# Encoder trunk on one core: other PSUM banks for one projection, another order of SBUF pools, another tail, and the inverse ahead of the stacks

## The chip, the cores and the metric

The kernel runs on one core of a Trainium2 chip. Its engines work side by side, each through its own list of instructions in order: TensorE (PE; the loading of its weights is shown apart as PEld), VectorE (DVE), ScalarE (ACT), GpSimd (POOL) and SyncE (SP), which only issues transfers. ACT and POOL issue transfers too. The metric is the time of one execution on the device in microseconds (us); lower is better.

## What is computed

A trunk of two layers over 1024 frames of width 1024, in float32. Layer 0 mixes by a recurrence (RWKV-7, 8 heads of 64) and by chunked band attention (8 heads of 64); layer 1 is a Conformer convolution module. Each layer ends with an MLP of squared ReLU, and the whole with an RMSNorm.

```python
for layer in range(DEPTH):
    h = rmsnorm(x, mix_norms[layer])
    if layer % 2 == 0:
        x = x + rwkv_attention_mixer(h, *mix_params[layer])
    else:
        x = x + conformer_conv(h, *mix_params[layer])
    g_ffn, up, down = ffn_params[layer]
    x = x + sq_relu_mlp(rmsnorm(x, g_ffn), up, down)
return rmsnorm(x, final_norm)
```

The mixer projects once for both groups; the recurrence holds a 64 x 64 state for each head, and the attention has a window of its own chunk and the eight before it:

```python
def step(S, inp):
    r_t, w_t, k_t, v_t, kk_t, a_t = inp
    sa = jnp.einsum('bhij,bhj->bhi', S, -kk_t)
    S = (S * w_t[:, :, None, :]
         + sa[..., None] * (kk_t * a_t)[:, :, None, :]
         + v_t[..., None] * k_t[:, :, None, :])
    y = jnp.einsum('bhij,bhj->bhi', S, r_t)
    return S, y
```

## The kernel before

**Layout.** Activations lie transposed, channels on the 128 partitions and frames along the row. The frames are worked in two halves of T = 512 (half 0 and half 1), each as 8 tiles of 128 x 512. Every large product is done in three steps for one: both operands are split into a rounded part and a rest (`xh` and `xl`, `wh` and `wl`), and `xh*wh`, `xl*wh` and `xh*wl` are summed in PSUM. All these steps go through `dense` (L141, matmul at L144). Weights come from memory as `wr` (L250, four buffers), ACT rounds them to `wh` (L258) and DVE takes the difference `wl` (L259); `wh` and `wl` have the four buffers of pool `wp1` in the narrow part of the kernel and the eight of `wp2` in the wide part.

**Who sets the order.** A planner (the tile framework) lays out each engine's list when the kernel is built. It takes instructions that are ready by its own estimate of time, the one with the lowest priority number first. `At(name)` sets the class: "support" before "mixer" (the recurrence), "mixer" before "attn", "attn" before "dense". Dense steps thus fill what the others leave; they come in runs (`run_of`; 6 in the projections, 12 in the narrow MLP) whose later steps follow their head at once. A tile of a pool can be written when the planner has seen the release of the buffer's last user, and memory of a closed pool is reused by the pools opened after it, tile by tile.

**PSUM.** The narrow part has eight banks by name: d 2, w 2, v 1, c 1, a 2 (L1095). "d" is for the dense products, "w" for the preparation of the recurrence, "v" for its stacks and inverse, "c" for its chain, "a" for attention. The wide part has d 5, w 1, o 2 (L1161).

**Order of stages.** Input projection of half 0 (`w_in_gemm(0)`); then recurrence and attention of half 0 beside the input projection of half 1 (`w_in_gemm(1)`); then recurrence and attention of half 1 beside output projection and MLP of layer 0 for half 0. From L1159 on the kernel is wide: `glu(0)`, the convolution of half 0, `mixer_out(1)` and the MLP of half 1, and so on through layer 1; the last call is `ffn(xb, ...)` with the writer `Out(1, xb, up, True)`.

**Value projection.** The end of `w_in_gemm` (L421 to L437) makes the attention's values with frames on the partitions: four banks at once, one for each 128 frames, over eight steps of weights. The banks are those of `SPARE` (L266): d, d, a, a. In both halves; with half 0 "a" is free, with half 1 attention(0) uses "a" too.

**Recurrence.** A unit is a pair of heads in a block of 256 frames, eight units to a half. `prep` makes its operands, among them `bk` (keys and the like) and `vp` (values); in half 1 (`nbuf` = 2) there is one buffer of each, and also of `bkt` and `vs`. `stacks` (L698) turns `bk` on PE through bank "v" and copies it to `bkt` (L705, L706), then centres the values, also through "v", into `vs` (L710, L715). `invert` (L631) inverts four triangular 64 x 64 blocks: on DVE (L638 to L653), with two writes to and eight reads from DRAM on SP's queue (L660, L667), then by 16 and three times 16 small matmuls through bank "v" (L676, L688) into `xt`. `stage2` does the stacks, then the inverse, then `late`. `chain` (L725) walks through four chunks: it needs `xt`, `bkt` and `vs`. The loop of `rwkv` (L454 to L467) traces stage 3 of one unit, stage 2 of the next and stage 1 of the one after in turns.

**Wide pools.** L1161 opens, one above the other, `wp2` (split weights, 32 KB a partition), `mp2` (MLP's middle, 40 KB), `sx` (16 KB) and `up` (convolution: `dwt`, `halo`, `u`, `cv` and others, some 43 KB). Below them lay, from the bottom, `lop` and `wp1` (26 KB), `mp` (32 KB), and the pools of the recurrence and the attention of half 1.

**Tail.** `Out.add` runs behind each 128-channel tile of the last down product: ACT scales a copy (L1053), PE turns it back (L1059), ACT and DVE copy it to the output rows `u` (L1065, L1067). `Stat.add` squares each tile on ACT (L220) and adds it on DVE (L221). With the last tile, which is done in two halves of 256 frames, `write` (L1075) sums the squares over the partitions on PE (L1079), takes root and reciprocal (L1082, L1083), scales the output rows (L1089 on ACT, L1091 on DVE) and stores them from SP's queue (L1092).

## Time and profile before

| | us |
|---|---|
| median of 3 runs (lowest, highest) | 2415.16 (2414.27, 2418.61) |
| the profiled execution, its own time | 2409.59 |
| its span, first to last instruction | 2407.5 |
| PE busy in it | 2374.8 |
| DVE, ACT, POOL busy | 1706.2, 1198.9, 117.1 |
| mean granted TensorE clock | 0.998 |

A row of a table by line has: line, engine, operation, names out<-in, shapes, count, then busy us, mean ns of one, idle us of the engine just before, and what ended that idle time. A row in order of time has: start, length, engine, line and names, in brackets the idle time before. Rows of waits have: who waited, for whom, us in total, times, longest. A matmul's length is longer than its share of PE's time, since the next one starts before it ends; starts are what counts.

### The profile page before, as it was taken

The numbers are of one execution on the slowest core, as the hardware profiler recorded it, in microseconds if no ns is written. First come the engines' busy times: TensorE is split into PE (matmuls) and PEld (weight loads), VectorE is DVE, ScalarE is ACT, GpSimd is POOL, SyncE is SP. The second block draws the span as 40 slices with busy tenths as digits, with TensorE's granted clock in tenths as the row PEclk, the third lists the DMA queues.
The fourth block names the chain that finished last, engine by engine and source line by source line (L and its number), as shares of the span: only waits on it lengthen the run. The fifth ranks groups of instructions, "written<-read, shape, count | busy, mean of one in ns | idle before, by whom it ended". The sixth has DMA issues, their size and how long they took to land.

```text
span 2407.5 us, 37122 instructions
## 1 busy us (share of the span) xinstructions
PE 2374.8 (99%) x12804; PEld 1956.4 (81%) x12804; DVE 1706.2 (71%) x3575; ACT 1198.9 (50%) x2323; POOL 117.1 (5%) x243
## 2 busy tenths in 40 slices
PE   9999999899999999999999999999999999999998
PEld 7777777788888888888888888888888888888887
DVE  6787776587777764579999746799997465434434
ACT  6567666677676753434433335334333365423324
POOL 1120111100000000011000000000000000000000
PEclk9999999999999999999999999999999999999999
DMA  8574445633343323453333334433333334333332
GB/s 260 163 217 139 120 121 171 188 102 115 93 120 110 90 74 90 145 166 92 101 97 97 97 97 135 123 94 97 96 98 99 95 112 140 97 97 97 97 98 67
DMA packets 476042, 283.34 MB, mean 118 GB/s; under 512 B 44512, under 2 KB 453216, under 8 KB 475856
## 3 DMA queue, kind: packets, MB, share of 16 engines
q1 hardware_dynamic: 464976, 249.46, 35.7%
q0 software_dynamic: 9488, 30.28, 3.6%
q8 instruction: 101, 1.65, 0.3%
q10 hardware_dynamic: 1392, 1.24, 0.2%
q14 instruction: 85, 0.70, 0.1%
HBM read 247.31 MB, written 36.72 MB: 118 GB/s over the span
## 4 chain that ended last, share of the span: by engine, by line
PE 88%; DVE 4%; DMA 3%; ACT 3%; issue 1%; SPq 1%; ACTq 0%; DVEq 0%
PE d L144 77%; DMA pt<-pd 1%; PE a L160 1%; PE v L688 1%; PE a L883 1%; DVE wl L259 1%; PE a L144 1%; ACT wh L258 1%; PE a L861 1%; PE a L863 1%; PE c L746 1%; PE c L740 0%; DVE pr L650 0%; PE c L736 0%; PE v L676 0%
## 5 line engine op out<-in xcount | busy, mean ns | idle before, releaser
L258 ACT CAST wh<-wr 128x512 fp32r<-128x512 f32 x744 | 460.1, 620 | 922.9 <-PE d L144 839.0
L144 PE MATMUL d<-xh,wh 128*128 128x512 f32 x1872 | 745.6, 398 | 0.3 <-DVE t L408 0.2
L144 PE MATMUL d<-xh,wl 128*128 128x512 f32 x1872 | 730.7, 391 | 0.9 <-DVE wl L259 0.9
L144 PE MATMUL d<-xl,wh 128*128 128x512 f32 x1872 | 730.2, 390 | 0.0
L259 DVE TENSOR_TENSOR wl<-wr,wh 128x512 fp32r<-128x512 f32 x744 | 503.4, 687 | 197.5 <-ACT wh L258 142.2
L144 PEld LDWEIGHTS d<-xh,wl 128*128 128x128 f32 x1872 | 351.7, 188 | 76.4 <-DVE wl L259 1.3
L144 PEld LDWEIGHTS d<-xh,wh 128*128 128x128 f32 x1872 | 352.2, 188 | 70.0 <-issue 1.2
L144 PEld LDWEIGHTS d<-xl,wh 128*128 128x128 f32 x1872 | 352.3, 188 | 67.7 <-issue 0.5
L144 PE MATMUL d<-mh,wh 128*128 128x512 f32 (+1 forms) x1040 | 405.8, 390 | 0.0
L144 PE MATMUL d<-mh,wl 128*128 128x512 f32 (+1 forms) x1040 | 401.8, 386 | 0.0
L144 PE MATMUL d<-ml,wh 128*128 128x512 f32 (+1 forms) x1040 | 401.6, 386 | 0.0
L1014 DVE SCALAR_TENSOR_TENSOR cv<-u,dwt,cv 128x512 f32<-128x512 f32 x480 | 332.7, 749 | 0.7
L144 PEld LDWEIGHTS d<-mh,wl 128*128 128x128 f32 x1040 | 195.4, 188 | 40.0
L144 PEld LDWEIGHTS d<-ml,wh 128*128 128x128 f32 x1040 | 195.6, 188 | 37.6
L144 PEld LDWEIGHTS d<-mh,wh 128*128 128x128 f32 x1040 | 195.5, 188 | 37.7
L913 DVE TENSOR_TENSOR x<-d,x 128x512 f32<-128x512 f32 (+1 forms) x146 | 97.8, 681 | 152.1 <-PE d L144 151.6
L955 DVE SCALAR_TENSOR_TENSOR t<-d,rstd 128x512 f32<-128x512 f32 x128 | 86.6, 688 | 114.6 <-PE d L144 111.9
L961 DVE TENSOR_TENSOR ml<-t,mh 128x512 fp32r<-128x512 f32 x128 | 87.9, 689 | 12.6 <-ACT mh L959 9.5
L957 ACT ACTIVATE t<-t 128x512 f32<-128x512 f32 x128 | 80.0, 625 | 12.2 <-DVE t L955 11.2
L959 ACT ACTIVATE mh<-t 128x512 fp32r<-128x512 f32 x128 | 78.9, 616 | 0.0
L745 ACT ACTIVATE sd<-vs,dc 64x64 f32<-64x64 f32 x128 | 44.1, 345 | 40.7 <-DVE vs L749 29.6
L221 DVE TENSOR_TENSOR acc<-acc,t 128x512 f32<-128x512 f32 (+1 forms) x86 | 58.0, 675 | 8.4 <-ACT t L220 8.3
(271 smaller groups left out, 2335.0 us busy)
## 6 DMA issues: line engine op xcount, KB each, us to landing
wr<-in_up_dram SPq DMA_DIRECT2D x256, 256.0 KB
wr<-in_dn_dram SPq DMA_DIRECT2D x256, 256.0 KB
wr<-in_w_in_dram SPq DMA_DIRECT2D x103, 256.0 KB
wr<-in_pw_dram SPq DMA_DIRECT2D x96, 256.0 KB
wr<-in_w_out_dram SPq DMA_DIRECT2D x32, 256.0 KB
pd<-t POOLq DMA_DIRECT2D x28, 256.0 KB, 2.6
x<-xd SPq DMA_DIRECT2D x24, 256.0 KB
pt<-pd SPq DMA_DIRECT2D x42, 128.5 KB
```

The lines of the kernel that those rows point to most:

```text
L144: ins = nc.tensor.matmul(*a, **k)
L160: ins = issue(*a, **k)
L221: nc.vector.tensor_tensor(out=self.acc[:, cols], in0=self.acc[:, cols], in1=sq[:, cols], op=ALU.add)
L258: nc.scalar.copy(hi[:], raw[:])
L259: nc.vector.tensor_tensor(out=lo[:], in0=raw[:], in1=hi[:].bitcast(F32), op=ALU.subtract)
L745: nc.scalar.activation(sd[hs[hd], :], sv[hs[hd], hd, c, :], AF.Copy, scale=dc[hs[hd], c : c + 1])
L913: nc.vector.tensor_tensor(out=xs[m][:, cols], in0=q[:, cols], in1=xs[m][:, cols], op=ALU.add)
L955: nc.vector.scalar_tensor_tensor(out=t[:], in0=q[:], scalar=0.0, in1=rstd[:], op0=ALU.max, op1=ALU.mult)
L957: nc.scalar.activation(sq[:], t[:], AF.Square)
L959: nc.scalar.activation(hi[:], t[:], AF.Square)
L961: nc.vector.tensor_tensor(out=lo[:], in0=sq[:], in1=hi[:].bitcast(F32), op=ALU.subtract)
L1014: nc.vector.scalar_tensor_tensor(out=c[:], in0=u[:, tap : tap + T], scalar=dw(tap), in1=c[:], op0=ALU.mult, op1=ALU.add)
```

## The change

Four edits. (A) In half 1 the value projection takes the banks d, d, v, c. (B) With `nbuf` = 2, that is in half 1, `stage2` runs the inverse ahead of the stacks. (C) The wide part opens its pools as `up`, `mp2`, `sx`, `wp2`. (D) In the tail the sum of squares is moved out of `write` into `sums`, which can add several parts; with the last tile of the last writer the square is made on DVE, is not added to the accumulator but summed beside it on PE, and `sums` is traced ahead of the turning back. There three of the four rows of a half are scaled on DVE and one on ACT, and two of the four are stored from ACT's queue.

```diff
--- before.py
+++ after.py
@@ -419,7 +419,7 @@
         run_of(RUN[0])
         gemm(w_in, 0, IN_ORDER, rhs, evac, st, first, mark=h)
         run_of(RUN[2])
-        qs = [psum(tag) for tag in SPARE]
+        qs = [psum(tag) for tag in (SPARE if h == 0 else ("d", "d", "v", "c"))]
         for k in range(KT):
             with boost():
                 hi, lo = (a[:].rearrange("p a b -> p (a b)")
@@ -785,8 +785,12 @@
             nc.gpsimd.dma_start(yd[hp][:, t0 : t0 + RT], yc[:])
 
         def stage2(u):
-            yield from stacks(u)
-            yield from invert(u)
+            if nbuf > 2:
+                yield from stacks(u)
+                yield from invert(u)
+            else:
+                yield from invert(u)
+                yield from stacks(u)
             late(u)
 
         def stage3(u):
@@ -919,14 +923,19 @@
 
         gemm(w, row0, range(KT), rhs, evac, taper=taper, after=after, halves=halves)
 
-    def norm_collect(xs, gname):
+    def norm_collect(xs, gname, final=False):
         st = Stat()
         rhs = [None] * KT
 
         def last(m, cols):
             if gname is not None:
                 rhs[m] = split(xs[m][:], m, v(gname, m))
-            st.add(xs[m][:], cols)
+            if final and m == KT - 1:
+                sq = tmp("t2")
+                nc.vector.tensor_tensor(out=sq[:, cols], in0=xs[m][:, cols], in1=xs[m][:, cols], op=ALU.mult)
+                st.rest = sq
+            else:
+                st.add(xs[m][:], cols)
 
         return st, rhs, last
 
@@ -942,7 +951,7 @@
         return nrhs, st
 
     def ffn(xs, rhs, rst, up, dn, mp, nxt, out_to=None, late=None):
-        st, nrhs, last = norm_collect(xs, nxt)
+        st, nrhs, last = norm_collect(xs, nxt, out_to is not None and out_to.final)
         if out_to is not None:
             out_to.st = st
         groups = DFF // D
@@ -1051,9 +1060,11 @@
         def add(self, m, cols):
             n = tmp("t1")
             nc.scalar.activation(n[:, cols], self.xs[m][:, cols], AF.Copy, scale=v("gf", m))
-            q = psum("o")
             c2, j = divmod(m, 4)
             ts = range(cols.start // P, cols.stop // P)
+            if self.final and m == KT - 1:
+                self.sums([self.st.acc, self.st.rest], ts)
+            q = psum("o")
             for t in ts:
                 with At("dense"):
                     nc.tensor.transpose(q[:, t * P : (t + 1) * P], n[:, t * P : (t + 1) * P], ident)
@@ -1068,28 +1079,34 @@
             if self.final and m == KT - 1:
                 self.write(ts)
 
-        def finish(self):
-            with boost():
-                self.write(range(4))
-
-        def write(self, ts):
+        def sums(self, parts, ts):
             q = psum("o")
-            for t in ts:
+            pairs = [(part, t) for part in parts for t in ts]
+            for i, (part, t) in enumerate(pairs):
                 with At("dense"):
-                    nc.tensor.matmul(q[:, t : t + 1], self.st.acc[:, t * P : (t + 1) * P], ones[:, 0:1], start=True, stop=True)
+                    nc.tensor.matmul(q[:, t : t + 1], part[:, t * P : (t + 1) * P], ones[:, 0:1],
+                                     start=(i == 0), stop=(i == len(pairs) - 1))
             w = slice(ts[0], ts[-1] + 1)
             r = self.r
             nc.scalar.activation(r[:, w], q[:, w], AF.Sqrt, bias=kc[:, 0:1], scale=1.0 / D)
             nc.vector.reciprocal(out=r[:, w], in_=r[:, w])
-            for c2 in range(2):
-                for t in ts:
-                    rows = slice(self.h * T + t * P, self.h * T + (t + 1) * P)
-                    o = self.o[4 * c2 + t][:, 0:T]
-                    if t % 2:
-                        nc.scalar.activation(o, o, AF.Copy, scale=r[:, t : t + 1])
-                    else:
-                        nc.vector.tensor_scalar(o, o, r[:, t : t + 1], None, op0=ALU.mult)
-                    nc.sync.dma_start(out[rows, c2 * T : (c2 + 1) * T], o)
+
+        def finish(self):
+            with boost():
+                self.sums([self.st.acc], range(4))
+                self.write(range(4))
+
+        def write(self, ts):
+            r = self.r
+            for i, (c2, t) in enumerate((c2, t) for c2 in range(2) for t in ts):
+                rows = slice(self.h * T + t * P, self.h * T + (t + 1) * P)
+                o = self.o[4 * c2 + t][:, 0:T]
+                if i == 1 if self.final else t % 2:
+                    nc.scalar.activation(o, o, AF.Copy, scale=r[:, t : t + 1])
+                else:
+                    nc.vector.tensor_scalar(o, o, r[:, t : t + 1], None, op0=ALU.mult)
+                queue = nc.scalar if self.final and i in (1, 2) else nc.sync
+                queue.dma_start(out[rows, c2 * T : (c2 + 1) * T], o)
 
 
     with banks(d=2, w=2, v=1, c=1, a=2), tc.tile_pool(name="lop", bufs=1) as lop, tc.tile_pool(name="wp1", bufs=4) as wb[0]:
@@ -1158,7 +1175,7 @@
 
     wide[0] = True
     run_of(1)
-    with banks(d=5, w=1, o=2), tc.tile_pool(name="wp2", bufs=8, reuse_waits="tile") as wb[0], tc.tile_pool(name="mp2", bufs=10, reuse_waits="tile") as mp, tc.tile_pool(name="sx", bufs=4, reuse_waits="tile") as extra[0], tc.tile_pool(name="up", bufs=1, reuse_waits="tile") as up:
+    with banks(d=5, w=1, o=2), tc.tile_pool(name="up", bufs=1, reuse_waits="tile") as up, tc.tile_pool(name="mp2", bufs=10, reuse_waits="tile") as mp, tc.tile_pool(name="sx", bufs=4, reuse_waits="tile") as extra[0], tc.tile_pool(name="wp2", bufs=8, reuse_waits="tile") as wb[0]:
         dwt = up.tile([P, KT * TAPS], F32, tag="dwt", name="dwt")
         nc.scalar.dma_start(dwt[:], vecs[:, VOFF["dw"] : NVEC])
         halo = up.tile([P, KT, TAPS - 1], F32, tag="halo", name="halo")
```

## What was forecast before the run

> **What bounds the kernel now.** I read the page's busy times first, then the same by stretches, then the engines' order in time where a stretch shows idle TensorE, because an engine that is busy 99% of the span leaves only its idle time, and slow-clocked time, to win.
>
> ```profile
> span 2407.5 us, 37122 instructions
> PE 2374.8 (99%) x12804; PEld 1956.4 (81%) x12804; DVE 1706.2 (71%) x3575; ACT 1198.9 (50%) x2323; POOL 117.1 (5%) x243
> ```
>
> The table by stretches has start and end, length, busy time of PE, PEld, DVE, ACT and POOL with counts, the granted PE clock, DMA share and GB/s.
>
> ```profile
> 300.00:420.00 120.00, 117.41 (x910) 94.34 (x910) 85.46 (x288) 81.64 (x204) 17.16 (x39) 1.00 0.49 147
> 429.50:436.50 7.00, 6.48 (x31) 4.91 (x29) 2.31 (x5) 5.66 (x11) 1.08 (x2) 1.00 0.72 214
> 436.50:445.90 9.40, 5.31 (x41) 3.75 (x41) 2.12 (x9) 3.91 (x8) 0.54 (x1) 0.88 0.37 145
> 445.90:464.50 18.60, 17.88 (x76) 14.45 (x77) 12.53 (x25) 12.08 (x24) 3.18 (x12) 0.97 0.61 188
> 480.00:960.00 480.00, 476.51 (x3296) 393.05 (x3296) 341.52 (x978) 314.35 (x660) 18.04 (x52) 1.00 0.35 99
> 1028.50:2399.00 1370.50, 1370.45 (x6159) 1136.47 (x6157) 978.83 (x1566) 535.59 (x920) 26.08 (x24) 1.00 0.35 103
> ```
>
> From 1028.5 to 2399 us PE is idle for 0.05 us: 6159 matmuls in 1370.5 us, 0.2225 us each, and nothing but fewer matmuls could shorten that. In 480 to 960, where the recurrence and the attention of half 1 run with layer 0's MLP between them, only 3.5 us of 480 are idle. The hole is 436.5 to 445.9: 4.1 us of 9.4 are idle and the clock there is 0.88. So the change is worth what it does in three places: that hole, the seam to the wide part near 1027, and the tail after 2399.
>
> **Edit A, banks of the value projection in half 1.** In order of time (start, length, engine, line, in brackets the idle time before and what ended it):
>
> ```profile
> 436.55 0.88 PE L160 MATMUL a<-pT,vt 128*64 128x128 f32 x12 [0.57 <-ACT pT L884]
> 441.89 1.27 PE L883 MATMUL a<-cst,pt 128*128 128x128 f32 x8 [3.32 <-ACT pt L874]
> 443.88 1.97 PE L160 MATMUL a<-pT,vt 128*64 128x128 f32 x16 [0.73 <-ACT pT L884]
> 445.79 0.80 PE L144 MATMUL a<-wh,xh 128*128 128x512 f32 x1
> 446.38 0.63 PE L144 MATMUL a<-wh,xl 128*128 128x512 f32 x1
> 446.81 0.53 PE L144 MATMUL a<-wl,xh 128*128 128x512 f32 x1
> 447.17 0.39 PE L144 MATMUL a<-wh,xh 128*128 128x512 f32 x1
> ```
>
> PE waits three times for the last softmax of attention(0), and right behind it the value projection goes on in banks "a" (names in `a<-wh,xh`). It owns two "a" banks by its list and can't get them before attention(0) lets go; its two "d" banks had run ahead as far as the four buffers of split weights let them (24 of 48 steps before 436). In the changed list the other two banks are "v" and "c". Their users in half 0 are done earlier; the last reader of "c" there is the gate product (`e<-e,c`), and the first user of "v" in half 1 comes at 481.8.
>
> ```profile
> 427.78 0.42 DVE L784 TENSOR_TENSOR e<-e,c 128x256 f32<-128x256 f32 x1
> ...
> 481.80 0.55 PE L705 MATMUL v<-cst,bk 128*128 128x128 f32 x3
> ```
>
> So from 428.2 us all four banks are free, and 96 steps of 0.2225 us, 21.4 us of dense work that has the lowest priority, stand ready to fill the hole. Attention(0) itself ends no earlier: its steps are a chain through ACT and DVE.
>
> What goes: 0.57 + 3.32 + 0.73 = 4.62 us idle. And the clock: 0.12 x 9.4 + 0.03 x 18.6 = 1.7 us of lost clock in the two stretches. In rows: the 16 matmuls of 443.88 take 1.97 us where 12 took 0.88, so 16 should take 1.17: 0.8 lost; the three starts behind 445.79 are 0.59, 0.43 and 0.36 us apart instead of 0.2225: 0.7 lost. I take 1.5. Filling a hole is not perfect: with dense work at hand all the time, the stretch 300 to 420 still has 2.6 us of idle in 120, 0.022 per us, so 28 us (429.5 to 457.5) give 0.6 back. A = -(4.62 + 1.5) + 0.6 = **-5.5 us**; ends -6.1 and, if the planner places no step in the hole, 0.
>
> The Trainium skill ("TensorE: Matmul & The Clock Gate", Part 1: The HAM clock gate) says the array's clock falls to half after an idle window of about 3.4 us and returns after as long a busy one. The granted clock agrees here: the idle time was 3.32 us and 1.7 us of clock were lost behind it. Without that rule the sum would have the 4.62 us alone.
>
> What is late next: the projection ends near 464.5 - 6 = 458.5 instead of 464.5, and the output projection of half 0 must be ready to take over.
>
> ```profile
> 449.76 0.37 SPq L938 DMA_DIRECT2D mh<-yd  x1
> 465.92 0.69 DVE L189 TENSOR_TENSOR xl<-mh,xh 128x512 fp32r<-128x512 f32 x1 [0.38 <-ACT xh L188]
> ```
>
> ```profile
> pd<-t POOLq DMA_DIRECT2D x28, 256.0 KB, 2.6
> ```
>
> The last attention tile is reloaded at 449.8, and its split at 465.9 waits not for it but for the projection to free the eighth input buffer. With as long a way as the page gives for a 256 KB store, 2.6 us, it is there by 452.5, six us ahead of need. The casts and differences of the weights for the last four steps (4 x 1.3 us on ACT and DVE) now fall into the softmax and may put attention(0) back by 1 to 2 us; the 6 us cover that.
>
> **Edit B, the inverse ahead of the stacks in half 1.** No instruction is added or removed. The end of one unit's stacks (L710) and inverse (from L676), and then the next unit:
>
> ```profile
> 623.37 0.71 PE L710 MATMUL v<-cent,vp 128*128 128x128 f32 x4
> 628.88 0.68 PE L676 MATMUL v<-e,g 64*64 64x64 f32 x16
> 641.20 0.63 PE L705 MATMUL v<-cst,bk 128*128 128x128 f32 x4
> 666.32 0.44 DVE L670 STREAM_TRANSPOSE e<-xdt 128x256 f32<-128x256 f32 x1
> 676.77 0.38 PE L746 MATMUL c<-vs,bkt 128*128 128x128 f32 x2
> 677.38 0.59 ACT L706 COPY bkt<-v 128x512 f32<-128x512 f32 x1
> 685.34 0.68 PE L676 MATMUL v<-e,g 64*64 64x64 f32 x16
> ```
>
> The transposed keys sit in the only "v" bank from 641.2 to 678, because their copy needs the only buffer `bkt`, which the chain of the unit before reads until L746. The inverse has its input at 666.8 but starts on PE at 685.3. The inverse's ten DMAs (L660, L667) and its DVE part lie before 666 and wait for none of this, so SP's queue keeps its order; the stacks issue no DMA. What can move is 16 + 3 x 16 small matmuls, by up to 18.5 us, per unit. That shortens a latency of the recurrence, which is not what bounds the stretch: PE is full of dense matmuls there, and the recurrence ends 70 us before the dense work it hides behind (last stores of each):
>
> ```profile
> L785 POOL DMA_DIRECT2D yd<-e x16: 539/539/542, 164.7 to 957.3; - x16
> 1027.95 0.50 PE L144 MATMUL d<-xh,wl 128*128 128x512 f32 x1 [0.93 <-DVE wl L259]
> ```
>
> B = **0**; ends: -3.5 (all idle of 480 to 960 gone) and +3.5 (that idle doubled).
>
> **Edit C, order of the wide pools.** The second row above is the seam: the first split weights of the pointwise convolution are late by 0.93 us, since their buffers lie at the bottom of the freed memory, over those of the narrow part that are in use until the last down product. On top they lie over attention(1)'s and the end of the recurrence's tiles, free by 957. At the bottom now lie `dwt`, `halo` and the `u` tiles; POOL's eight copies into `u` (L995) must now wait for the last product near 1027, with the stores of x (L908) in the same queue behind or ahead of them. DVE writes the first `u` only when the first four column blocks are nearly through, 1.75 x 48 x 0.2225 = 19 us later, and the x tiles are reused after all sixteen, 16 x 24 x 0.2225 = 85 us, so 19 us cover it. C = **-0.9**; ends -0.9 and +1.
>
> **Edit D, the tail.**
>
> ```profile
> 2399.00 0.42 DVE L913 TENSOR_TENSOR x<-d,x 128x256 f32<-128x256 f32 x1 [0.84 <-PE d L144]
> 2399.52 0.42 ACT L220 ACTIVATE t<-x 128x256 f32<-128x256 f32 x1 [1.69 <-DVE x L913]
> 2400.39 0.44 PE L1059 MATMUL o<-cst,t 128*128 128x128 f32 x2 [1.42 <-ACT t L1053]
> 2400.66 0.50 PE L1079 MATMUL o<-ones,acc 128*128 128x1 f32 x4
> 2401.20 0.26 ACT L1082 ACTIVATE orst<-o,small 128x2 f32<-128x2 f32 x1
> 2401.49 0.17 DVE L1083 RECIPROCAL orst<-orst 128x2 f32<-128x2 f32 x1
> 2401.70 1.33 ACT L1089 ACTIVATE u<-u,orst 128x512 f32<-128x512 f32 x2 [0.23 <-DVE orst L1083]
> 2401.70 0.88 DVE L1091 TENSOR_SCALAR u<-u,orst 128x512 f32<-128x512 f32 x2
> 2402.21 1.78 SPq L1092 DMA_DIRECT2D out_dram<-u  x4
> ```
>
> Now the square of the last half tile goes to DVE (0.43, 2399.43 to 2399.86) while ACT starts the scaled copy at once; sums of the accumulator need nothing late, those of the square start near 2399.9 and, four short passes of 0.12 us later, Sqrt can run at 2400.4 instead of 2401.2. So the first scaled tile is ready 0.8 us earlier, and the first DMA goes out near 2401.4. The transfers follow: 1 MB, which moves in 2.8 us behind the first issue.
>
> ```profile
> GB/s 0 0 0 0 0 0 0 0 101 374 359 388 402 360 388 402 359 402 331 374 431 402 359 388 402 359 388 331 58 0 0 0 0 0 0 0 0 0 0 0
> ```
>
> (40 slices of 2401.8 to 2407.5 us.) One 256 KB piece takes 0.7 us and SP issues one per 0.45, so the last issue isn't what decides; the first one is: -0.8. Four more short passes for the sums of the first half lie on PE's path: +0.2 (a fourth of four at 0.12 is hidden). D = **-0.6**; ends -1.3 (two queues also pack the issues closer) and +0.3 (DVE, which has one scaling more, becomes last). The Trainium skill ("Trainium Kernel Development and Optimization", Key Constraints) speaks against the second queue: DMAs of several queues share 16 engines, and issuing from two saves only issue time. The row at 360 to 400 GB/s without a break agrees; by it D stays -0.6, without it the queue alone might give another -0.7.
>
> **Sum.** -5.5 + 0 - 0.9 - 0.6 = -7.0 us. The profiled execution took 2409.59 us, 2.1 over its span, and lies 5.6 under the median of the three runs, 2415.16. So its like would be 2402.6, and the median **2408.2 us**, -0.29%.
>
> **The rivals.** (1) *The hole stays or moves*: the planner orders PE by its own clock; if it keeps the steps behind attention(0), or ACT and DVE give the casts their turn too late, A is 0 to -2.5 and the sum -1.5 to -4: 2411 to 2413.7. For it: inside the projection PE also waits for a step of the recurrence, with dense work about. Against: 300 to 420 shows the same kinds of steps filled.
>
> ```profile
> PE w L543 <- DVE xl L525: 0.7, 1, 0.7
> ```
>
>  (2) *B does nothing that it says*: the planner takes whatever is ready, the stacks' input is there by 641, the inverse's at 666.8, so L705 may take "v" first as before. About even; the time is the same, 2408. (3) *Slower*: if the inverse does get "v" first, `bk` and `vp`, one buffer each in half 1, are held until the stacks behind it have read them, and the next unit's preparation waits. A unit takes (957 - 464.5) / 8 = 62 us; it may grow by 70 / 8 = 8.7 us before the recurrence outlasts the dense work; beyond that each us costs 8. By the rows a round from L710 (623.4) to L670 (666.8) is 43, the inverse's PE part (628.9 to 641.2, when "v" is free) 12, the stacks 3: 58, so it isn't due. At 14 us more the cost is 42 and the time 2450. A milder form, the 3.5 us idle of half 1 grown to the 0.022 per us of 300 to 420, gives +7 and 2415.
>
> **Chances.** Forecast case, with (2) inside it: 0.72 (2404 to 2410.3: all ends of B, C and D on the good side give -11). Rival 1 and a mild loss in B: 0.21. Rival 3: 0.07. With 0.2%, 4.8 us, about what a measurement of this kernel can tell from no change: faster 0.72, same 0.20, slower 0.08. The range 2403 to 2414.5 leaves out the slower case and the worst of the mild ones; the likeliest case alone is 2404 to 2410.3.
>
> **What would show it.** A: no PE idle over 1 us between 429 and 465, no half clock there, `v<-wh,xh` and `c<-wh,xh` groups, the projection done by 459. B: L676 before L706 in half 1 if rival 2 is wrong; the last L785 between 900 and 1000 either way. C: no wait for `wl` at the seam. D: the first store of the last piece of output 0.8 us closer to the last L913. Wrong: idle time over 8 us in 465 to 1020, or a second stretch at half clock.

## The result, and the profile after

| | before | after |
|---|---|---|
| median, us (4 runs of each, one chip) | 2415.95 | 2439.51 |
| after / before, with its 95% interval | | 1.0100 (1.0081 to 1.0118) |
| span of the profiled execution, us | 2407.5 | 2435.1 |

The change makes the kernel about 1% slower, 23.6 us by the medians. The forecast was 2408.2 us, with slower at a chance of 0.08.

The page of the changed kernel, first the span and the busy times:

```profile
span 2435.1 us, 37116 instructions
...
PE 2398.1 (98%) x12812; PEld 1957.6 (80%) x12812; DVE 1712.1 (70%) x3577; ACT 1195.2 (49%) x2319; POOL 108.1 (4%) x243
```

The span is 27.6 us longer, and PE is busy for 23.3 us more with eight matmuls more. So most of the loss is not idle time: PE spends longer over the same work. The table by stretches says where (start and end, length, busy us and counts of PE, PEld, DVE, ACT, POOL, granted PE clock, DMA share, GB/s):

```profile
429.50:436.50 7.00, 7.00 (x36) 5.51 (x32) 4.93 (x15) 4.12 (x8) 1.61 (x3) 1.00 0.54 154
436.50:445.90 9.40, 9.40 (x53) 7.43 (x52) 5.54 (x15) 5.62 (x14) 1.08 (x2) 1.00 0.90 309
445.90:464.50 18.60, 18.60 (x97) 14.99 (x96) 8.21 (x17) 11.12 (x22) 3.81 (x11) 1.00 0.51 164
480.00:960.00 480.00, 469.03 (x3221) 386.31 (x3221) 338.41 (x970) 311.93 (x649) 15.44 (x42) 1.00 0.35 98
1034.00:2427.00 1393.00, 1392.99 (x6168) 1137.72 (x6167) 982.97 (x1564) 531.35 (x914) 19.13 (x33) 1.00 0.34 101
```

The hole before 464.5 us is full, at full clock: part A does there what it says. In 480 to 960 PE is idle for 480 - 469.03 = 11.0 us, before for 3.5. And the wide part has no idle time and full clock in both kernels, yet 6168 matmuls now take 1393 us where 6159 took 1370.5.

Both kernels run the same 8976 dense steps in the same order, but for nine in the seam whose products come in another order, so the starts of the same steps divide both spans into pieces that can be compared, whatever stands between. From the traces, in us (the first of the later experiments stands beside them):

```
dense steps     what lies there                    before    after   c_aligned
start to 0                                           11.0     12.3     11.0
0 to 1151       half 0, to the value projection     418.2    419.8    421.9
1151 to 1248    value projection of half 1           35.2     27.2     27.3
1248 to 2950    recurrence, attention of half 1     556.0    568.7    570.4
2950 to 3072    seam to the wide part                30.3     29.6     29.1
3072 to 8975    wide part                          1347.9   1369.2   1347.8
8975 to end     tail                                  8.8      8.2      8.1
```

A takes 8.1 us out of the projection, the seam gives 0.7 and the tail 0.6. Against that stand 12.7 us in the recurrence of half 1, where the forecast had B at 0 with ends of 3.5, and 21.3 us in the wide part, where it had no term at all. Each column is one execution, and that of the kernel before (2409.59 us) lies 6 us under its median, that of the changed kernel 2 under its own, so the pieces add up to more than the medians' 23.6. Five kernels with the same lists as before up to 2950 (before and the four with pads below) differ by 2.8 us in the row 1248 to 2950 (556.0 to 558.8).

In a stretch in which PE never idles in either kernel, first before, then after (columns as above):

```profile
1240.00:2380.00 1140.00, 1140.00 (x5082) 943.97 (x5081) 769.93 (x1227) 441.62 (x758) 8.60 (x12) 1.00 0.35 102
```

```profile
1240.00:2380.00 1140.00, 1140.00 (x4999) 930.02 (x4998) 772.49 (x1220) 431.09 (x737) 8.59 (x12) 1.00 0.35 102
```

83 matmuls fewer in the same time: 228.0 ns each instead of 224.3. By operands, between 1240 and 1320 us (operation, names, count: shortest, median and longest duration in ns, start of the first and the last), before:

```profile
L144 PE MATMUL d<-xh,wh x64: 389/389/389, 1258.9 to 1301.8; 128*128 128x512 f32 x64
...
L144 PE MATMUL d<-mh,wl x55: 389/389/389, 1239.7 to 1319.9; 128*128 128x512 f32 x55
```

and after:

```profile
L144 PE MATMUL d<-xh,wh x64: 389/392/398, 1270.3 to 1314.3; 128*128 128x512 f32 x64
...
L144 PE MATMUL d<-xl,wh x64: 389/394/402, 1270.6 to 1314.5; 128*128 128x512 f32 x64
...
L144 PE MATMUL d<-xh,wl x64: 387/399/399, 1270.8 to 1314.7; 128*128 128x512 f32 x64
...
L144 PE MATMUL d<-mh,wl x52: 387/389/389, 1240.2 to 1319.6; 128*128 128x512 f32 x52
```

The 64 rounds of three steps on `xh` and `xl` go from 42.9 us between first and last start to 44.0, while the steps on `mh` and `ml` keep their 389 ns. The instructions are the same; only where the tiles lie in SBUF has changed.

The layout of the built programs shows it. `wp2`, `mp2` and `sx` were the first pools of the wide part and began at multiples of 128 bytes. Now `up` lies below them, and with `dwt` of 992, `halo` of 960, eight `u` tiles of 2168 (2176 each with what the allocator adds) and 24,576 bytes of other tiles it is 43,936 bytes long, 343.25 times 128. So the weights, the MLP's middle and the extra split tiles in `sx` now begin 32 bytes behind a multiple of 128. The other `xh` and `xl` tiles, in the older pool `spool`, begin at multiples of 128 as before. The steps that got slower are those that multiply a tile of the one kind by a tile of the other: 2736 of the 5904 from step 3072 on. By their starts they come every 234 ns on average, those on `mh` and `ml` every 227.

### The profile page after: what moved, and what is told of

It is laid out like the page before. It is cut to its first block, busy times and chain, and to the rows that moved or that the text cites. A ratio compares the mean times of both kernels' runs of the same rounds, so it can differ in the third digit from the quotient of the medians.

```text
span 2435.1 us, 37116 instructions
## 1 busy us (share of the span) xinstructions
PE 2398.1 (98%) x12812; PEld 1957.6 (80%) x12812; DVE 1712.1 (70%) x3577; ACT 1195.2 (49%) x2319; POOL 108.1 (4%) x243
## 4 chain that ended last, share of the span: by engine, by line
PE 84%; DVE 5%; DMA 3%; ACT 3%; issue 1%; SPq 1%; DVEq 0%; POOL 0%; ACTq 0%; POOLq 0%
PE d L144 74%; DMA pt<-pd 1%; PE a L160 1%; PE v L688 1%; DVE wl L259 1%; PE a L887 1%; PE a L865 1%; ACT wh L258 1%; PE c L746 1%; DVE pr L650 0%; DMA nb<-msc 0%; PE a L867 0%; PE c L740 0%; DMA xdt<-xsc 0%; PE c L736 0%
## 5 line engine op out<-in xcount | busy, mean ns | idle before, releaser
L144 PE MATMUL d<-xh,wl 128*128 128x512 f32 x1872 | 739.6, 395 | 0.1
L917 DVE TENSOR_TENSOR x<-d,x 128x512 f32<-128x512 f32 (+1 forms) x146 | 97.6, 679 | 142.1 <-PE d L144 141.8
```

The source lines that it names most:

```text
L144: ins = nc.tensor.matmul(*a, **k)
L917: nc.vector.tensor_tensor(out=xs[m][:, cols], in0=q[:, cols], in1=xs[m][:, cols], op=ALU.add)
```

## The experiments

Each kernel ran beside the kernel before on the same chip; ratios are to those runs.

### Is it the offset?

`c_aligned` is the changed kernel with three kinds of tiles of `up` rounded up to 128 bytes, as `whole` does for others of this kernel. PE, DVE, ACT and SP have the same lists as in the changed kernel.

```diff
-        dwt = up.tile([P, KT * TAPS], F32, tag="dwt", name="dwt")
+        dwt = up.tile([P, whole(KT * TAPS)], F32, tag="dwt", name="dwt")
...
-        halo = up.tile([P, KT, TAPS - 1], F32, tag="halo", name="halo")
+        halo = up.tile([P, KT, 32], F32, tag="halo", name="halo")[:, :, 0 : TAPS - 1]
...
-            u = up.tile([P, T + TAPS - 1], F32, tag="u", name="u", bufs=8)
+            u = up.tile([P, whole(T + TAPS - 1)], F32, tag="u", name="u", bufs=8)
```

> The changed kernel with the rows of dwt, halo and u rounded up to 128 bytes, so that every tile of the wide pools begins at a multiple of 128 bytes; the engines' lists stay as they are. Theory 'offset' (the dense steps of the wide part are slower because the weights begin 32 bytes off a multiple of 128 while xh and xl begin on one): the 21 us lost behind 1060 us come back, pitch of xh steps 227 ns again, time 2418 (2416 to 2420). Rival 'place' (the weights now lie at the top of SBUF, far from xh, or in a place that other traffic crosses): nothing comes back, pitch stays 232 to 237, time 2438 to 2440.

`shift32` is the kernel before, with a pad of 32 bytes below the wide pools:

```diff
-    with banks(d=5, w=1, o=2), tc.tile_pool(name="wp2", ...
+    with banks(d=5, w=1, o=2), tc.tile_pool(name="pad", bufs=1) as pad, tc.tile_pool(name="wp2", ...
+        nc.gpsimd.memset(pad.tile([P, 8], F32, tag="pad", name="pad")[:], 0.0)
```

> The kernel before with one tile of 32 bytes opened below the wide pools, so that wp2, mp2 and sx lie 32 bytes higher in the old order and the old place. Theory 'offset': the steps with xh and xl from the narrow part's pool run at 232 to 237 ns, +21 us, time 2437. Rival 'place': no change, 2416 within 2.

Measured: `c_aligned` 2413.44 us against 2413.29, ratio 0.9998 (0.9985 to 1.0011); `shift32` 2433.73 us, ratio 1.0086 (1.0070 to 1.0102). The offset alone makes the wide part slow. Putting it back takes away the wide part's loss (1347.8 us, before 1347.9), and by the medians the change as a whole is then even with the kernel before, 2.6 us under the 2416 at which my range for `c_aligned` began. Which pool lies where, and which waits for whose memory, has no part in the wide part's loss. In the steady stretch `c_aligned` does 5077 matmuls and `shift32` 5006:

```profile
1240.00:2380.00 1140.00, 1140.00 (x5077) 943.70 (x5076) 773.97 (x1231) 440.04 (x752) 8.60 (x12) 1.00 0.35 103
```

```profile
1240.00:2380.00 1140.00, 1140.00 (x5006) 931.43 (x5006) 770.69 (x1218) 432.04 (x738) 8.59 (x12) 1.00 0.35 102
```

### Whose offset, and how fine?

Three pads in the kernel before: `weights32` moves only the weights (a pad of 32 bytes ahead of `wp2`, one of 96 behind it), `others32` only `mp2` and `sx` (32 bytes behind `wp2`), `shift64` everything by 64 bytes.

```diff
# weights32
+ tc.tile_pool(name="pad", bufs=1) as pad,   # 32 bytes
  tc.tile_pool(name="wp2", bufs=8, ...) as wb[0],
+ tc.tile_pool(name="pad2", bufs=1) as pad2, # 96 bytes
# others32
  tc.tile_pool(name="wp2", bufs=8, ...) as wb[0],
+ tc.tile_pool(name="pad", bufs=1) as pad,   # 32 bytes
# shift64
+ tc.tile_pool(name="pad", bufs=1) as pad,   # 64 bytes
  tc.tile_pool(name="wp2", bufs=8, ...) as wb[0],
```

> The kernel before with the weight tiles of the wide part alone moved by 32 bytes; the tiles that move through the array (xh, xl, mh, ml) all stay at offset 0. Theory 'relative offset' (a step is slow when the two operands of a matmul stand at different offsets): now the steps with mh and ml are slow as well, all 5903 steps of the wide part by some 5.7 ns, +34 us (30 to 42), about 2447. Rival 'own offset of the weights': steps with xh and xl slow, those with mh and ml at 227 ns as in the changed kernel, +20 us, about 2434.

> The kernel before with its weight tiles at offset 0 and the tiles of mh, ml (and of the extra split tiles) moved by 32 bytes. Theory 'relative offset': steps with mh and ml go to 232 to 237 ns, those with xh and xl in their old tiles stay at 227, about 2300 of the 5903 steps by 5.7 ns, +13 us (10 to 21), about 2427. Rival 'own offset of the weights': nothing changes, within 3 us of the kernel before.

> The kernel before with a pad of 64 bytes below the pools of the wide part (shift32 had 32 bytes and cost 20.4 us). Theory 'what counts is the offset within 128 bytes': dense steps with xh or xl stay at 232 to 237 ns, time about 2434. Rival 'what counts is the offset within 64 bytes': all dense steps of the wide part at 227 ns, time that of the kernel before within 3 us.

| kernel | us, before beside it | ratio (95%) | wide part, 3072 to 8975, us |
|---|---|---|---|
| weights32 | 2450.31, 2414.83 | 1.0153 (1.0137 to 1.0169) | 1386.2 |
| others32 | 2435.04, 2414.83 | 1.0091 (1.0072 to 1.0109) | 1370.4 |
| shift64 | 2433.90, 2414.83 | 1.0079 (1.0061 to 1.0098) | 1367.0 |

With the weights alone moved, the steps on `mh` are slow too. Between 1240 and 1320 us:

```profile
L144 PE MATMUL d<-xh,wh x64: 392/395/398, 1273.4 to 1317.5; 128*128 128x512 f32 x64
...
L144 PE MATMUL d<-mh,wl x50: 399/399/399, 1240.2 to 1319.4; 128*128 128x512 f32 x50
```

With the weights in their place and `mh`, `ml` moved, it is the steps on `mh` that are slow, and most of those on `xh` are not:

```profile
L144 PE MATMUL d<-xh,wh x64: 389/389/402, 1266.5 to 1309.8; 128*128 128x512 f32 x64
...
L144 PE MATMUL d<-mh,wl x52: 393/396/397, 1239.7 to 1319.4; 128*128 128x512 f32 x52
```

So it isn't the weights' own offset: a step is slow when its two operands start at different offsets. Two operands both at 32 run at full pace, as `mh` does in the changed kernel. 64 bytes apart costs as much as 32 (19.1 and 20.4 us), so what counts is not the offset within 64 bytes; I count it within 128, and no larger measure was tried. `others32` came out at +20.2 us where I expected +13, the top of my range being 21. I had left out that 816 of the 3552 steps on `xh` and `xl` use tiles that lie in `sx` and moved too, hence the slow ones among the first row's, and a step costs nearer 7 ns than the 5.7 that I took.

### What A gives alone, and where it goes

`a_only` is the kernel before with part A alone.

```diff
-        qs = [psum(tag) for tag in SPARE]
+        qs = [psum(tag) for tag in (SPARE if h == 0 else ("d", "d", "v", "c"))]
```

> The kernel before with edit A alone (banks d, d, v, c). Theory as forecast, seen in the changed kernel's trace as -8.1 us over the 97 steps around the projection: no idle time and no half clock between 430 and 465, time 2408 (2406 to 2411). Rival: the gain of the changed kernel came from its other list of instructions and is lost later, time 2414 to 2418.

Measured: 2411.78 us against 2413.29, ratio 0.9995 (0.9985 to 1.0005), between the theory's range and the rival's. The projection is 8.0 us shorter (27.2 us for 35.2), but the piece behind it takes 564.0 us for 556.0: the gain is given back at once. PE's waits between 460 and 1000 us in this kernel (who waited, for whom, us in total, times, longest):

```profile
PE w L543 <- DVE xl L525: 2.4, 2, 1.5
PE a L883 <- ACT pT L884: 1.8, 1, 1.8
PE w L160 <- DVE bv L598: 1.4, 1, 1.4
```

The first is 0.7 us in the kernel before, the second 0.5, the third 0.4. What made `xl` late is seen on ACT, in order of time (start, length, engine, line, in brackets the idle time before and what ended it):

```profile
455.78 1.26 ACT L436 ACTIVATE t<-d,rc 128x512 f32<-128x512 f32 x2
...
460.51 0.49 ACT L488 ACTIVATE e<-pt,vec 128x256 f32<-128x256 f32 x1
462.50 0.69 ACT L436 ACTIVATE t<-v,rc 128x512 f32<-128x512 f32 x1 [1.49 <-DMA vd<-t]
463.08 0.39 ACT L524 CAST xl<-e 64x256 fp32r<-64x256 f32 x1
463.38 0.68 ACT L436 ACTIVATE t<-c,rc 128x512 f32<-128x512 f32 x1
...
464.91 0.40 ACT L524 CAST xl<-e 64x256 fp32r<-64x256 f32 x1
```

The four banks are evicted through two buffers `t`. The third eviction waits until the first has been stored; ACT works in order, so the loras' rounding (L524) stands behind it, and behind that DVE's difference (L525) and PE's L543. Before, the third and fourth eviction came at 467.5 and 469.4 us, behind L524, so their waits for stores held nothing up there:

```profile
457.14 0.81 ACT L524 CAST xl<-e 64x256 fp32r<-64x256 f32 x2
...
467.55 0.69 ACT L436 ACTIVATE t<-a,rc 128x512 f32<-128x512 f32 x1 [0.37 <-DMA vd<-t]
469.38 0.69 ACT L436 ACTIVATE t<-a,rc 128x512 f32<-128x512 f32 x1 [1.14 <-DMA vd<-t]
```

The third wait is of the same kind on DVE: A makes the output projection's tiles early enough for their eight splits (L192) to come ahead of the recurrence's L593 and L598 (before, these ran at 508.0 and 511.9 us and the splits from 520.4 on):

```profile
516.78 4.06 DVE L192 SCALAR_TENSOR_TENSOR xl<-x,vec,xh 128x512 fp32r<-128x512 f32 x6
...
524.61 0.47 DVE L593 SCALAR_TENSOR_TENSOR e<-e,vec 128x256 f32<-128x256 f32 x1
```

And the clock falls to half behind two of the waits, at 465.6 and 527.0 us, as it fell before at 443.7. Part of the 8 us is only moved: L543 and L544, four small matmuls that with their wait took 1.5 us inside the projection before, at 458.3, now stand behind it.

Next, the change without B, on its right offsets (`acd_aligned`), and the same with the third and fourth eviction into tiles of another tag (`acd_evict`):

```diff
-                s = tmp("t1")
+                s = tmp("t1" if t < 2 or h == 0 else "t2")
                 nc.scalar.activation(s[:], q[:], AF.Copy, scale=st.part[1][:, t : t + 1])
```

> The changed kernel with its tiles back on 128-byte offsets and without part B (A, C and D stay). Theory 'the parts add up': A alone gave -1.5 us and B alone +3.8 us against the kernel before, the changed kernel with the offsets put back gave 0.15 us more than before, so this one is at c_aligned less B's price: 3 to 4 us below the kernel before, about 2409.7; the projection of half 1 ends by 459 us, the idle time between 460 and 960 us stays at 8 to 10 us as in A alone. Rival 'B stood in A's way': without B the 8 us that A closes are kept, and the time is 8 us or more below, about 2405.

> acd_aligned (the change without B, on 128-byte offsets; 4 us below the kernel before) with the third and fourth eviction of the value projection of half 1 into tiles of another tag (t2), so that they need not wait for the stores of the first two. Theory 'ScalarE behind a store': the wait of L436 for the store of t (2.4 us at 462 in acd_aligned) goes, the loras' splits behind it come that much earlier, TensorE's 2.4 us of idle time at 464 to 468 us before L543 goes, and with it 2 to 4 us: 6 to 8 us below the kernel before. Rival 'the idle time moves on': the wait at L436 goes, but idle time of as much appears elsewhere before 1000 us, and the time stays 3 to 5 us below the kernel before.

Measured: `acd_aligned` 2410.80 us against 2414.83, ratio 0.9983 (0.9974 to 0.9992); `acd_evict` 2404.03 us against 2412.93, ratio 0.9962 (0.9950 to 0.9973). The first lies 4.0 us below, as the theory of adding parts said (3 to 4); the second gains more than the 6 to 8 expected. On ACT the four evictions no longer wait for a store, and the loras' rounding is over by 461.9:

```profile
456.76 0.69 ACT L436 ACTIVATE t<-v,rc 128x512 f32<-128x512 f32 x1
...
457.85 0.69 ACT L436 ACTIVATE t<-c,rc 128x512 f32<-128x512 f32 x1
...
461.08 0.82 ACT L524 CAST xl<-e 64x256 fp32r<-64x256 f32 x2
```

The wait of L543 for L525 is gone. But others come in its place (PE's two longest between 459 and 560 us):

```profile
PE a L861 <- DMA kk<-pl: 1.7, 1, 1.7
PE a L883 <- ACT pt L874: 1.2, 1, 1.2
```

The piece from step 1248 to 2950 takes 557.7 us, within 1.7 of the kernel before, while the projection keeps its 8 us. This is the fastest kernel of the study, 8.9 us below the kernel before. To see whether the tiles or merely another list of the planner did it, the same edit with A alone (`a_evict`) and with the whole change (`abcd_evict`):

> The kernel before with part A and with the third and fourth eviction of half 1's value projection into tiles t2. A alone gave -1.5 us; in the change without B the other tiles gave 5 us more. Theory 'ScalarE behind a store': A's gain comes through, 5 to 8 us below the kernel before, about 2407. Rival 'a fortunate list': -3 to 0 us, as A alone.

> The whole change (B too) with its tiles on 128-byte offsets and the same two evictions into t2. c_aligned, the same without the t2 tiles, stood 0.15 us above the kernel before. Theory 'ScalarE behind a store': 4 to 6 us below the kernel before, about 2409. Rival 'a fortunate list': within 3 us of the kernel before.

Measured: `a_evict` 2407.32 us against 2413.54, ratio 0.9970 (0.9958 to 0.9982); `abcd_evict` 2409.90 us, ratio 0.9986 (0.9974 to 0.9999). By the medians' distance to the kernel before, the two tiles gave 8.9 - 4.0 = 4.9 us in the change without B, 6.2 - 1.5 = 4.7 us with A alone and 3.6 + 0.15 = 3.8 us with the whole change. The whole change lies just short of its 4 to 6, but all three point one way, so the edit itself is worth some 4 to 5 us, with no B and with it. That the store's wait at L543 alone carried the loss isn't shown. Idle PE by stretch, in us, without and with the other tiles, says that the time comes back later:

```
us               a_only  a_evict   acd_aligned  acd_evict   c_aligned  abcd_evict
460 to 480          2.4      2.4           2.6        2.1         2.2         2.0
480 to 540          4.3      2.5           3.6        1.8         1.4         2.5
540 to 960          3.0      2.6           3.1        1.9        10.1         6.1
```

Between 460 and 480, where PE waited at L543, there is about as much idle time as without the edit, now for `kk` and `pt`. The gain lies behind 480: with A alone and without B where L160 waited for `bv`, with the whole change behind 540. Whether the earlier rounding brought that about or the planner's other list did stays open.

### What B costs

`b_only` is the kernel before with part B alone.

```diff
-            yield from stacks(u)
-            yield from invert(u)
+            if nbuf > 2:
+                yield from stacks(u)
+                yield from invert(u)
+            else:
+                yield from invert(u)
+                yield from stacks(u)
```

> The kernel before with edit B alone (the inverse ahead of the stacks in half 1). Theory: B by itself costs what the changed kernel lost between the projection and the seam, 12.7 us (9.4 of them idle time, 1.7 half clock), through units that come one behind another through the single buffers bk and vp: time 2426 to 2430, last store of the recurrence 35 to 45 us later. Rival: the loss came from A and B together (the recurrence started under another list), B alone costs 0 to 4, time 2416 to 2420.

Measured: 2417.06 us against 2413.29, ratio 1.0013 (1.0002 to 1.0025). It costs about 4 us, inside the rival's range and far from the theory's 12.7: the piece from 1248 to 2950 is 5.7 us longer with B alone and 8.0 with A alone, together about the 12.7 of the changed kernel and the 14.4 of `c_aligned`. The inverse does get bank "v" first, in the changed kernel as well, and the units get longer: from one `xt` to the next 58.9 us on average, before 53.4; the recurrence's last store comes at 1006.6 us, before at 957.3. In the trace the loop behind that is plain. Starts in us of the same steps of one unit:

```
                                        before    b_only
values out of vp (L710), unit n          571.3     601.1
vp written again, unit n+1               572.5     601.9
bv, unit n+1                             585.9     608.4
masked products (L160), unit n+1         588.6     610.7
fold, the inverse's first step           600.6     624.2
inverse on PE (L676)                     628.9     643.1
xt (L696)                                640.2     649.6
values out of vp (L710), unit n+1        623.4     656.8
```

Before, the values leave `vp` 17 us ahead of the unit's own `xt`; with B they leave it behind. The next unit's whole preparation waits for `vp` and `bk`, so preparation, inverse and stacks of successive units no longer overlap. Three kernels tried this: half of B with the values behind the inverse (`b_keys_first`), the other half with the keys behind it (`b_values_first`), and the first with a second `vp` (`b_keys_first_v2`), for which the inverse's tile `e2` gives up one of its two buffers.

```diff
# stacks split into stack_k (L705, L706) and stack_v (L710, L715); with nbuf = 2:
-            yield from stacks(u)
-            yield from invert(u)
+            yield from stack_k(u)      # b_values_first: stack_v
+            yield from invert(u)
+            yield from stack_v(u)      # b_values_first: stack_k
# b_keys_first_v2 also:
-            vp = rp.tile([P, RT], F32, tag="vp", name="vp", bufs=nbuf - 1)
+            vp = rp.tile([P, RT], F32, tag="vp", name="vp", bufs=2)
...
-            xn = e("e2", 2)
+            xn = e("e2", nbuf - 1)
...
-                    rhs = blk(e("e2", 2)[:])
+                    rhs = blk(e("e2", nbuf - 1)[:])
```

> The kernel before with half of B in half 1: the turned keys ahead of the inverse, as before, the turned values behind it. B whole cost +3.8 us and made the time from one chain's start to the next 59.0 us instead of 54.6. Theory 'held buffer': the values' one buffer (vp) is held until the turned values are out, the next unit's bv, masked products and inverse wait for it, and so half of B closes the same loop: 58 to 59 us a unit, +3 to +4 us. Rival 'work in between': the stacks merely lie between inverse and chain, so half the stacks cost half: 56 to 57 us a unit, about +2 us.

> The other half of B: the turned values ahead of the inverse, the turned keys behind it. Theory 'held buffer': now bk, single as well, is held until behind the inverse, and the next unit's products wait for it: 57 to 59 us a unit, +3 to +4 us. Rival 'work in between': 56 to 57 us a unit, about +2 us, and the two halves add up to the whole of B.

> b_keys_first with two buffers for vp in half 1 (the inverse's tile e2 gives one of its two for it). Theory 'held buffer': the loop is open again, at most 56 us a unit, within 1.5 us of the kernel before. Rival 'work in between': as b_keys_first, whatever that is.

| kernel | `xt` to `xt`, us | ratio to before (95%) |
|---|---|---|
| b_only | 58.9 | 1.0013 (1.0002 to 1.0025) |
| b_keys_first | 58.0 | 1.0010 (0.9999 to 1.0021) |
| b_values_first | 55.7 | 1.0039 (1.0025 to 1.0052) |
| b_keys_first_v2 | 51.9 | 1.0023 (1.0014 to 1.0032) |

For the length of a unit the held buffer holds: with `vp` held it is 58.0, with a second `vp` 51.9, less than before the change. `b_values_first` at 55.7 fits the rival better. For the time neither theory holds: the kernel with the shortest units costs no less than B whole (the intervals overlap), and one with units in between costs most. The length of a unit doesn't decide the time; PE idles for 6.7 to 9.1 us between 480 and 960 in these four, in a dozen or so waits of 0.2 to 1.8 us at changing places. So the question became whether any other list costs as much. `run10` and `run14` are controls that change nothing but the length of the dense runs in this stretch; `b_run10` and `b_run14` add B:

```diff
-RUN = 6, 12, 6
+RUN = 6, 10, 6      # run14: 6, 14, 6
```

> The kernel before with dense runs of 10 steps instead of 12 in the stretch where the mixer of half 1 runs (RUN[1]); nothing else. A control. Theory 'B's order costs by itself': within 2 us of before. Rival 'the list of before is a lucky one': +3 to +9 us, with 4 to 8 us more idle time between 460 and 960 us, as in the kernels with B.

> run10 with part B. Theory 'B's order costs by itself': 3 to 6 us above run10. Rival 'the list of before is a lucky one': within 2 us of run10.

> As run10 with dense runs of 14 steps: a second control. Theory 'B's order costs by itself': within 2 us of before. Rival 'the list of before is a lucky one': +3 to +9 us.

> run14 with part B. Theory 'B's order costs by itself': 3 to 6 us above run14. Rival 'the list of before is a lucky one': within 2 us of run14.

Ratios to before, idle PE between 480 and 960 us (480 less PE's busy time in that stretch) and the units, these two from one execution of each kernel:

```
list                    without B                                with B
                        ratio (95%)               idle  unit     ratio (95%)               idle  unit
before, runs of 12      1                          3.5  53.4     1.0013 (1.0002, 1.0025)    9.1  58.9
runs of 10              1.0014 (1.0004, 1.0024)    7.5  46.2     1.0013 (1.0002, 1.0024)    6.8  54.3
runs of 14              1.0031 (1.0019, 1.0043)    8.4  53.5     1.0028 (1.0015, 1.0040)    8.1  57.2
A, C, D aligned         0.9983 (0.9974, 0.9992)    6.7  54.8     0.9998 (0.9985, 1.0011)   11.5  58.8
the same, t2 tiles      0.9962 (0.9950, 0.9973)    3.7  53.9     0.9986 (0.9974, 0.9999)    8.6  60.0
```

The rows of `run10` and of `b_run10` for that stretch:

```profile
480.00:960.00 480.00, 472.50 (x3276) 388.97 (x3276) 343.52 (x981) 317.11 (x662) 17.95 (x52) 1.00 0.35 99
```

```profile
480.00:960.00 480.00, 473.25 (x3275) 387.63 (x3274) 341.61 (x976) 308.93 (x653) 15.45 (x42) 1.00 0.35 98
```

By the ratios, controls that leave the units' order alone cost 3.4 and 7.5 us, and B on top of them costs nothing. In the three other lists B costs 0.13 to 0.24%. So the list of the kernel before is one with little idle time among its neighbours, and B loses that as a change of run length does; every list with B has over 6 us idle, those without have 3.5 to 8.4. Whether the order itself adds something to that, and which wait would carry it, stays open: five pairs, three one way and two neither, don't settle it.

## Why the prediction was wrong

**Edit C, the step that failed.** I wrote C as -0.9 with ends -0.9 and +1, from the waits of POOL's copies and of the weights at the seam. That part was right: no wait for `wl` is left between 1000 and 1060 us, and the seam is 0.7 us shorter (1.2 in `c_aligned`). What I never priced was that moving a pool also moves the start of every tile above it. I took the pace of the wide part, 0.2225 us a matmul, as fixed ("nothing but fewer matmuls could shorten that"); it depends on the two operands' addresses, and 5903 dense steps at 3.6 ns more on average are the 21.3 us. No rival had it.

**Edit A.** In its place the mechanism held: the hole is filled and no clock is lost there. The projection is 8.1 us shorter where I took 5.5 with an end of 6.1, but the 1.5 us of L543 and L544, with their wait of 0.72 us, only moved behind it, to 465.6. The 6.6 that are left are more than the term, which counted the slow time low: the 46 small matmuls that stay in the piece took 5.9 us and now take 4.1, where I had 0.8 to gain. The execution that I read was even a mild one: there half clock lasted 3.41 us behind the hole and the projection 35.2 us, in the twelve later kernels with the old banks 6.83 us or more and 35.8 to 36.8 us.

The step of this term that failed is that it stopped at 464.5. What came behind has the size of the rival "the hole stays or moves", which I gave 2411 to 2413.7 (A alone measured 2411.78), though the hole didn't stay as that rival had it: it was filled, and other waits came later. I had asked what is late next and looked at PE's inputs from the output projection. Late were ACT's small casts, behind an eviction that waited for a store, and DVE's L593, behind the splits; and the third and fourth bank of the projection are named in the very edit. With the other tiles for these two A gives 6.2 us.

**Edit B.** Rival 2, that the planner would leave the order, was wrong: L676 came ahead of L705. Rival 3 named the right buffers, `bk` and `vp`, and its round of 58 us was close to the 58.9 measured. What it had wrong was the 62 us that it held this against: that was the stretch from 464.5 to 957 divided by eight, with the first unit's preparation in it, while from one `xt` to the next a unit took 53.4. By its own 58 the units were due to grow by 4.6. They grew by 5.5, less than the 8.7 that it allowed, and the recurrence did end ahead of the dense work. The ends of +-3.5 us were too narrow: idle time in 480 to 960 went from 3.5 to 9.1 us with B alone and to 11.0 in the changed kernel, and the one long wait there is followed by half clock (stretches of 3.4 us before and behind 796.94):

```profile
793.52:796.94 3.42, 1.21 (x6) 1.08 (x7) 3.19 (x15) 0.90 (x3) 0.00 (x0) 1.00 0.18 51
796.94:800.35 3.41, 3.41 (x9) 2.64 (x9) 2.41 (x9) 0.11 (x1) 0.54 (x1) 0.50 0.63 195
```

The "milder form" of rival 3, +7 us of idle time, was the right size by a rule of thumb; that was luck. The last store of the recurrence came at 997.5 us, inside the 900 to 1000 I gave:

```profile
L785 POOL DMA_DIRECT2D yd<-e x16: 539/539/542, 169.4 to 997.5; - x16
```

**Edit D.** Forecast -0.6, measured -0.6 (8.8 to 8.2 us behind the last dense step's start; the other kernels with D have 8.1 three times and 8.8 once). The first store leaves 2429.81 - 2427.18 = 2.63 us behind the last L917, before 3.21 behind L913, so 0.58 us closer where I said 0.8. The +0.2 for the added passes doesn't show either (the wide part takes 1347.8 us in `c_aligned`, 1347.9 before), so the total is right by two small misses that cancel. The sums of the square start 0.94 us behind L917 where the sums started 1.66 behind L913:

```profile
2427.18 0.42 DVE L917 TENSOR_TENSOR x<-d,x 128x256 f32<-128x256 f32 x1 [0.25 <-PE d L144]
2427.64 0.43 DVE L935 TENSOR_TENSOR t<-x 128x256 f32<-128x256 f32 x1
...
2428.12 0.61 PE L1087 MATMUL o<-ones,t 128*128 128x1 f32 x4 [0.64 <-DVE t L935]
...
2429.81 1.29 SPq L1109 DMA_DIRECT2D out_dram<-u  x2
```

**Range and chances.** With the offsets put back, the whole change stands at 2413.44 us, inside my range, which ended at 2414.5. But that range stood against a median of 2415.16; the kernel before took 2413.29 beside `c_aligned`, so the change is worth +0.15 us there, where the range meant -12.2 to -0.7. Even without the offsets the loss behind A and in B left nothing of the forecast's -7.0. (A small slip: the good ends add up to -11.8 and 2403.4, not to -11 and 2404.) Both signs that I had named for "wrong" came: idle time over 8 us behind 465, and a second stretch at half clock.

## What to carry to other kernels

When an edit reorders or resizes pools, list the start of every matmul operand modulo 128 bytes before and after: two operands that differ there made a 128x512 step about 3% longer here, with PE busy all the time and nothing to see in the waits. A gain that closes a hole counts only when the next thing late has been sought on every in-order engine; here one such thing was an eviction that waited for a store ahead of small casts that PE needed. And where a planner sets the order, a result within 0.3% needs a control that merely rearranges the list.

## What was not expected of the hardware

**Pace by relative offset.** A 128x512 step started every 227 ns when its moving tile and its weights began at the same offset modulo 128 bytes (0 and 0, or 32 and 32), and every 234 ns on average (most between 231 and 238) when they began 32 or 64 bytes apart; the loads of the weights took 188 ns either way. Whether it is the two reads that collide, and what other distances do, was not tried. The Trainium skill ("SBUF — State Buffer", Operand start alignment) says of starting addresses only what is legal, a multiple of the element size, and that its runs timed nothing; all the tiles here are legal by it.

**Half clock behind little idle time, and not always.** In `a_only` PE was busy for 2.21 of 3.43 us, and the next 3.41 us were granted half the clock:

```profile
523.60:527.03 3.43, 2.21 (x14) 1.60 (x12) 3.36 (x11) 2.56 (x5) 0.00 (x0) 1.00 0.76 223
527.03:530.44 3.41, 3.15 (x22) 2.93 (x23) 2.83 (x11) 2.68 (x4) 0.00 (x0) 0.50 0.57 163
```

The window ends in a wait of 1.45 us, the longest there. The Trainium skill ("TensorE: Matmul & The Clock Gate", Part 1: The HAM clock gate) speaks of an idle window of about 3.4 us; in these rows a window of that length that is one third idle came ahead of half clock, with small matmuls in the rest. Idle time alone doesn't settle it, though. The half clocks of one execution start a whole number of 3.413 us apart, and in the kernel before, of two such windows ahead of 443.67 the first has more idle time than the one above and full clock follows:

```profile
436.84:440.25 3.41, 1.73 (x16) 0.93 (x12) 1.79 (x7) 0.55 (x1) 0.54 (x1) 1.00 0.91 356
440.26:443.67 3.41, 1.27 (x8) 0.83 (x8) 0.33 (x2) 3.19 (x8) 0.00 (x0) 1.00 0.03 11
443.67:447.08 3.41, 3.19 (x19) 2.67 (x20) 0.29 (x1) 0.16 (x1) 0.55 (x2) 0.50 0.00 0
```

What decides is not shown here. The lengths agree with that window: ahead of the tail half clock lasts 3.41 us, twice that (6.83) or, in `weights32`, three times (10.24).
